# Packing, gated heads and merged branches moved between the weight blocks of a hybrid decoder layer

## The chip, the cores and the metric

The kernel runs on one core of a Trainium2 chip. The time is the device's, in microseconds, of one execution; the figure to be predicted is the median of several executions. TensorE (PE) does the matmuls, VectorE (DVE) and ScalarE (ACT) casts, sums and activations, GpSimd (POOL) and SyncE (SP) issue DMAs. Each engine works its own instructions in order and waits on semaphores of the others.

## The reference

One layer, x of 256 rows and 4096 columns, all in fp32:

- pre-RMSNorm, then one projection `hn @ w_in`, whose 18336 columns are split among two attention branches, two gate paths (2048 columns each) and two merge gates (`merge_a`, `merge_b`, 4096 columns each);
- branch A (latent attention) and branch B (sparse attention with an indexer) give `o_a` and `o_b`, 256 x 2048 each, multiplied by the SiLU of their gates;
- `merged = sigmoid(merge_a) * (o_a @ p_a) + sigmoid(merge_b) * (o_b @ p_b)`;
- the result is `x + merged @ w_o`.

The weights are 4096 x 18336 (`w_in`), 2048 x 4096 (`p_a`, `p_b`) and 4096 x 4096 (`w_o`), beside two smaller ones.

## The kernel before

Every fp32 matrix is split into two fp32r parts, `hi` (a cast on ACT) and `lo` (the rest, a subtraction on DVE), and a product is three matmuls of 128 x 128 by 128 x 512: hi by hi, lo by hi, hi by lo (`mm3`, lines 105 to 108). So each block of weights is loaded by SP, cast by ACT, subtracted by DVE, and then multiplied by PE.

**The streams** (`run_streams`). Up to 1215 us the columns of `w_in` for the branches and gates, and the first 1024 of `merge_a`, go through PE in streams of 512 columns. A stream has 16 weight units of two 128-row tiles; one unit is 12 matmuls for the two halves of x. At a unit the casts and subtractions of the unit two ahead are issued (`hi_part`, `lo_part`; three buffers of each, so a cast waits until PE has released a buffer), and the load of the one six ahead (four buffers). After the first tile of a unit a hook `each(u)` may issue more work. The last two streams, `done_ma(0)` and `done_ma(1)`, are the first 1024 columns of `merge_a`; their results go through a sigmoid on ACT (L1096) and by POOL to `sig_d` in HBM (L1087).

**The wide units.** From there on work is a list `sched` of units, written out by `block(w, c0, order, end)`: an order is a list of unit names, 1024 columns wide.

- `p5` is a plain unit: weight rows of tiles 10 and 11, four quarters (two halves of the rows, two of the columns) x 2 tiles x 3 = 24 matmuls.
- `s4` does the tiles 8 and 9 with Strassen's products: 7 x 3 = 21 matmuls. It needs sums of the weights (three DVE operations, L1195 to L1197, into `wsum`, a single buffer) and more casts; and sums of the left matrix, which were "packed" before: for each chunk `c` of four 128-row tiles, `a_sums` (L1070 to L1073) makes three sums and overwrites one quarter, and the sums are split into `xh`, `xl`. An s unit of tiles 2p, 2p+1 uses chunk p/2.
- `g` loads gated heads of a branch from `go_d`, `m` merged columns from `mt_d`, both through the weights' ring, and split two chunks into the tiles `h` and `l` that held x or the heads before; `m` also packs. `d` does that for the last merged columns, straight from SBUF. `t` transposes the merged result of a p_a/p_b block (16 short matmuls, four ACT copies). None of g, m, d has matmuls of its own.

The order of work is written out by hand. For unit i (`run_wide`), DVE's and ACT's work of unit i+2 is issued first (`prep`), then SP's loads of units i+3 to i+5 (`raw_dma`, a ring `wraw` of three buffers of 1 MB, used by s, p, g and m), then PE's products of unit i, then the block's `end`. Of `whi` and `wlo` there are three buffers, of `whs` and `wls` (for s units) two.

The blocks: seven of `w_in` (the rest of the merge gates; results through sigmoids to `sig_d`), alternately four of `p_a` and four of `p_b`, four of `w_o`. The gate blocks use x; the units of `p_a` use chunks 0 to 3 (g0, g1), those of `p_b` chunks 4 to 7 (g2, g3); those of `w_o` chunks 0 to 7 (m0: 0, 1; m1: 2, 3; m2: 4, 5; d3: 6, 7). In the last gate block g0 and g1 stand among the units; in the first p_a block g2 and g3; in the last p_b block m0 and m1; in the first w_o block m2, t3 and d3. POOL loads the sigmoids of a p block at its first unit (`on_first`, `load_sig`, 1 MB), into a buffer of `whs`.

**Packing x** for the gate blocks: `pack_x(c)`, at every second unit of the last stream (`each_pack`), one chunk at a time, in `wsum`. The sigmoids of the two merge streams are also written to `wsum`.

**The end.** A block has four accumulators for the quarters (`banks_c`) and four for Strassen's products (`banks_s`). `sets` says which are the four single-bank tiles ("c": `tr`, `tr`, `at`, `at`) and which the two tiles of two banks each ("s": `acc`). After the last s unit the Strassen products are summed (`sums_early`); after the last p unit each quarter is added (`sum_late`, L1257). In the last block x is added by an accumulating DMA of POOL (`add_x`, L1341) between the two, and each quarter leaves by SP as soon as it is added.

Of the kernel before, what the change touches and what calls it, by code (L numbers as in the profile page):

```python
# [9 lines left out]
F32 = mybir.dt.float32  # L10
F32R = mybir.dt.float32r
# [7 lines left out]
P = 128  # L19
# [18 lines left out]
def kernel(ctx: ExitStack, tc: tile.TileContext, x, positions, g_pre, w_in, g_q_lat,  # L38
# [79 lines left out]
    def flat(t):  # L118
        return t.rearrange("p a t -> p (a t)")
# [917 lines left out]

    F = {"h": xth, "l": xtl, "xh": [], "xl": []}  # L1040
# [16 lines left out]
    def sum_tiles(c):
        for q, lst in (("xh", F["xh"]), ("xl", F["xl"])):
            t = F["px"].tile([P, 3, P], F32R, name=f"{q}{c}")
            if len(lst) > c:  # L1060
                lst[c] = t
            else:
                lst.append(t)

    def a_sums(sums, a):

        v = nc.vector.tensor_tensor
        a11, a21, a12, a22 = (a[:, q * P:(q + 1) * P] for q in range(4))
        s1, s2, s4 = (sums[:, q, :] for q in range(3))
        v(s1, a21, a22, op=ALU.add)  # L1070
        v(a21, a21, a11, op=ALU.subtract)
        v(s2, s1, a11, op=ALU.subtract)
        v(s4, a12, s2, op=ALU.subtract)  # L1073

    def pack_x(c):

        t = flat(wsum())
        a, sums = t[:, 0:512], t[:, 512:896].rearrange("p (q t) -> p q t", q=3)
        nc.vector.tensor_tensor(a, flat(xth[c][:, 0:2, :]).bitcast(F32), flat(xtl[c][:, 0:2, :]).bitcast(F32),
                                op=ALU.add)  # L1080
        a_sums(sums, a)
        sum_tiles(c)
        split_w(xth[c][:, 0, P:], xtl[c][:, 0, P:], a[:, P:2 * P])
        split_w(F["xh"][c], F["xl"][c], sums)

    def out_sig(d, sg, b):
        nc.gpsimd.dma_start(sig_d[d][:, 512 * b:512 * b + 512].rearrange("(m p) c -> p m c", p=P), sg)  # L1087
# [1 line left out]
    def done_ma(b):  # L1089
        def done(acc):  # L1090
            if b == 0:
                yield from idle()
                open_wide()
            sg = wsum()[:, 0:2, :]
            for m in range(2):
                nc.scalar.activation(sg[:, m, :], acc[:, m, :], AF.Sigmoid, scale=r[:, m:m + 1])  # L1096
            release("acc")
            out_sig(0, sg, b)
            yield
        return done  # L1100

    def each_pack(u):
        if u % 2 == 1:
            pack_x(u // 2)


    for b in range(2):
        stream(stat_x, w_in, [(C_MA + 512 * b, 512)], done_ma(b), each=each_pack if b else None)


    sched = []
# [32 lines left out]
    def raw_dma(i):  # L1144
        if i >= len(sched) or i in asked:
            return
        asked.add(i)
        u = sched[i]
        kind, p, b = u["kind"], u["p"], u["b"]
        if kind not in "spgm":  # L1150
            return
        t = raws[i] = F["pa"].tile([P, 4, 512], F32, name="wraw", bufs=3)
        if kind in "gm":
            src = go_d[p // 2][:, 8 * (p % 2):8 * (p % 2) + 8, :] if kind == "g" else mt_d[:, 8 * p:8 * p + 8, :]
            nc.sync.dma_start(flat(t), src.rearrange("p k t -> p (k t)"))
            return
        for kk in range(2):
            q = 1 - kk if kind == "s" else kk
            row = (2 * p + kk) * P
            nc.sync.dma_start(flat(t[:, 2 * q:2 * q + 2, :]), b["w"][row:row + P, b["c0"]:b["c0"] + 1024])  # L1160

    def new_a(c):
        F["h"][c] = big.tile([P, 4, S], F32R, name=f"h{c}")
        F["l"][c] = big.tile([P, 4, S], F32R, name=f"l{c}")
        return F["h"][c], F["l"][c]

    def prep(i):

        if i >= len(sched) or i in his:
            return  # L1170
        u = sched[i]
        kind, p = u["kind"], u["p"]
        his[i] = None
        if kind == "t":
            return
        if kind in "gmd":
            raw = flat(F["merged_t"] if kind == "d" else raws[i])
            for q in range(2):
                c = (4 * (p // 2) + 2 * (p % 2) if kind == "g" else 2 * p) + q
                h, l = new_a(c)  # L1180
                a = raw[:, 1024 * q:1024 * q + 1024]
                if kind != "g":
                    sums = wsum()[:, 0, 0:384].rearrange("p (q t) -> p q t", q=3)
                    a_sums(sums, a)
                    sum_tiles(c)
                    split_w(F["xh"][c], F["xl"][c], sums)
                split_w(flat(h), flat(l), a)
# [90 lines left out]
    for n, (d, cb) in enumerate(gates):  # L1278
        order = mixed
        if n == 0:  # L1280
            order = "p1 p3 s0 p5 s2 p7 s4 p9 s6 p11 s8 s10 p13 s12 s14 p15".split()
        if n == len(gates) - 1:
            order = mixed[:6] + ["g0"] + mixed[6:10] + ["g1"] + mixed[10:]
        block(w_in, (C_MA, C_MB)[d] + 1024 * cb, order, end_sig(d, 1024 * cb))


# [48 lines left out]

# [21 lines left out]
    first_of = {}
    for i, u in enumerate(sched):
        if u["b"] is not None:
            first_of.setdefault(id(u["b"]), i)  # L1360

    def on_first(i, u):
        b = u["b"]
        if b["w"] is p_a or b["w"] is p_b:
            d = 0 if b["w"] is p_a else 1
            F["sig", d] = load_sig(d, b["c0"] // 1024)

    def run_wide():
        F["pb"] = ctx.enter_context(tc.tile_pool(name="wide2", bufs=1, side="right"))
        for i, u in enumerate(sched):  # L1370
            b = u["b"]
            if b is not None and first_of[id(b)] == i:
                on_first(i, u)
            prep(i + 2)
            for j in range(3, 6):
                raw_dma(i + j)
# [86 lines left out]
```

## Time and profile before

| | us |
|---|---|
| median of 3 executions | 2509.92 (2507.33 to 2510.38) |
| profiled execution, its own time | 2511.02 |
| its span, first to last instruction | 2509.1 |
| PE busy | 2476.4 (99%) |
| DVE busy | 1800.9 (72%) |
| ACT busy | 1318.7 (53%) |
| mean granted TensorE clock | 0.994 |

Matmuls overlap, so "PE busy" says that PE had something to do, not that it ran at full pace; the pace is seen in the number of matmuls of a stretch. The stretches: streams to about 1215 us, gate blocks to 1797, p_a and p_b to 2153, w_o to the end. In a row of the windows view the columns are the stretch, its length, and for each engine busy time and number of instructions, then the granted clock (1.00 is 2.4 GHz, 0.5 is 1.2), the DMA engines' share and GB/s. In a row of a timeline: start, duration, engine, line, operation, written and read tiles, shape, count, and in brackets the idle time of the engine before it and what ended it.

### The profile page before, as it was taken

The numbers are of one execution on the slowest core, as the hardware profiler recorded it, in microseconds if no ns is written. First come the engines' busy times: TensorE is split into PE (matmuls) and PEld (weight loads), VectorE is DVE, ScalarE is ACT, GpSimd is POOL, SyncE is SP. The second block draws the span as 40 slices with busy tenths as digits, with TensorE's granted clock in tenths as the row PEclk, the third lists the DMA queues.
The fourth block names the chain that finished last, engine by engine and source line by source line (L and its number), as shares of the span: only waits on it lengthen the run. The fifth ranks groups of instructions, "written<-read, shape, count | busy, mean of one in ns | idle before, by whom it ended". The sixth has DMA issues, their size and how long they took to land.

```text
span 2509.1 us, 31278 instructions
## 1 busy us (share of the span) xinstructions
PE 2476.4 (99%) x11790; PEld 2066.0 (82%) x11790; DVE 1800.9 (72%) x2086; ACT 1318.7 (53%) x1618; POOL 114.0 (5%) x159
## 2 busy tenths in 40 slices
PE   9999999999999999999999999999999999989998
PEld 7988888888888888887788888888788888768887
DVE  5676696655666666655899998999845456799996
ACT  6555545555665555553455555556533334455553
POOL 2000000000000000000000000000000000000000
PEclk9999999999999999999999999999999999999999
DMA  7655565565666666666556666666867666657775
GB/s 244 187 170 160 162 182 163 167 183 176 179 192 179 187 179 188 180 178 193 204 200 241 219 218 213 215 228 216 289 231 239 206 225 234 202 173 246 237 233 151
DMA packets 202790, 506.18 MB, mean 202 GB/s; under 512 B 25428, under 2 KB 38608, under 8 KB 201360
## 3 DMA queue, kind: packets, MB, share of 16 engines
q1 hardware_dynamic: 190816, 468.25, 59.2%
q0 software_dynamic: 11776, 35.93, 4.6%
q8 instruction: 92, 1.51, 0.2%
q14 instruction: 58, 0.48, 0.1%
q10 hardware_dynamic: 48, 0.02, 0.0%
HBM read 482.11 MB, written 22.02 MB: 201 GB/s over the span
## 4 chain that ended last, share of the span: by engine, by line
PE 83%; issue 9%; DMA 3%; DVE 3%; ACT 1%; SPq 0%; POOL 0%; DVEq 0%; ACTq 0%; POOLq 0%
PE acc L108 18%; PE acc L106 18%; PE acc L107 18%; PE at L108 4%; PE at L107 4%; PE at L106 4%; PE tr L106 4%; PE tr L107 4%; PE tr L108 4%; PE tr L129 2%; DVE wlo L1052 1%; DMA ev<-in_x 1%; DVE wls L1052 1%; DMA wraw<-in_p_a 1%; PE tr L615 0%
## 5 line engine op out<-in xcount | busy, mean ns | idle before, releaser
L237 DVE TENSOR_TENSOR lo<-raw,hi 128x1024 fp32r<-128x1024 f32 (+3 forms) x400 | 476.2, 1192 | 373.8 <-ACT hi L229 358.3
L1051 ACT CAST whi<-wraw 128x1536 fp32r<-128x1536 f32 (+1 forms) x240 | 419.6, 1755 | 458.9 <-PE at L107 232.2
L1052 DVE TENSOR_TENSOR wlo<-wraw,whi 128x1536 fp32r<-128x1536 f32 (+1 forms) x240 | 502.1, 2093 | 217.4 <-ACT whi L1051 217.1
L106 PE MATMUL acc<-hi,h 128*128 128x512 f32 (+1 forms) x1404 | 555.2, 395 | 2.4 <-ACT hi L229 1.9
L229 ACT CAST hi<-raw 128x1024 fp32r<-128x1024 f32 (+3 forms) x400 | 407.4, 1023 | 283.9 <-PE acc L107 256.7
L108 PE MATMUL acc<-lo,h 128*128 128x512 f32 (+1 forms) x1404 | 546.8, 389 | 0.5 <-DVE lo L237 0.5
L107 PE MATMUL acc<-hi,l 128*128 128x512 f32 (+1 forms) x1404 | 545.3, 388 | 0.8 <-DVE l L85 0.8
L108 PEld LDWEIGHTS acc<-lo,h 128*128 128x128 f32 x1404 | 263.8, 188 | 56.6 <-DVE lo L237 1.0
L106 PEld LDWEIGHTS acc<-hi,h 128*128 128x128 f32 x1404 | 264.0, 188 | 49.9 <-ACT hi L229 2.3
L107 PEld LDWEIGHTS acc<-hi,l 128*128 128x128 f32 x1404 | 264.3, 188 | 48.4 <-DVE l L85 1.1
L106 PE MATMUL acc<-whi,h 128*128 128x512 f32 x600 | 236.4, 394 | 7.4 <-DVE ev L1257 5.3
L108 PE MATMUL acc<-wlo,h 128*128 128x512 f32 x600 | 235.6, 393 | 3.2 <-DVE wlo L1052 3.2
L107 PE MATMUL acc<-whi,l 128*128 128x512 f32 x600 | 235.2, 392 | 0.0
L1051 ACT CAST whs<-wsum 128x1536 fp32r<-128x1536 f32 x88 | 130.3, 1480 | 119.4 <-DVE wsum L1196 119.3
L108 PE MATMUL tr<-wlo,h 128*128 128x512 f32 x440 | 171.4, 390 | 1.6 <-DVE wlo L1052 1.6
L106 PE MATMUL tr<-whi,h 128*128 128x512 f32 x440 | 171.7, 390 | 0.0
L107 PE MATMUL tr<-whi,l 128*128 128x512 f32 x440 | 171.6, 390 | 0.0
L1052 DVE TENSOR_TENSOR wls<-wsum,whs 128x1536 fp32r<-128x1536 f32 x88 | 154.2, 1752 | 1.2 <-PE acc L108 1.2
L106 PEld LDWEIGHTS acc<-whi,h 128*128 128x128 f32 x600 | 113.9, 190 | 32.9 <-DVE ev L1257 6.5
L106 PE MATMUL at<-whi,h 128*128 128x512 f32 x352 | 136.9, 389 | 0.0
L107 PE MATMUL at<-whi,l 128*128 128x512 f32 x352 | 136.9, 389 | 0.0
L108 PE MATMUL at<-wlo,h 128*128 128x512 f32 x352 | 136.9, 389 | 0.0
(333 smaller groups left out, 3480.8 us busy)
## 6 DMA issues: line engine op xcount, KB each, us to landing
raw<-in_w_in SPq DMA_DIRECT2D x335, 512.0 KB, 3.7
wraw<-in_w_in SPq DMA_DIRECT2D x224, 512.0 KB, 4.6
wraw<-in_w_o SPq DMA_DIRECT2D x128, 512.0 KB, 5.1
wraw<-in_p_a SPq DMA_DIRECT2D x64, 512.0 KB, 4.9
wraw<-in_p_b SPq DMA_DIRECT2D x64, 512.0 KB, 5.1
raw<-in_w_uq SPq DMA_DIRECT2D x32, 384.0 KB, 3.2
raw<-in_w_ukv SPq DMA_DIRECT2D x16, 512.0 KB, 4.1
whs<-sig_d POOLq DMA_DIRECT2D x16, 512.0 KB, 6.4
```

What stands on the lines that cost most here:

```text
L106: nc.tensor.matmul(o, ah, bh, start=start, stop=False)
L107: nc.tensor.matmul(o, al, bh, start=False, stop=False)
L108: nc.tensor.matmul(o, ah, bl, start=False, stop=stop)
L129: nc.tensor.transpose(tr[:, a * S + m * P:a * S + (m + 1) * P], src_of(a, m), ident)
L229: nc.scalar.copy(t[:, ks, :width(i)], raws[i][:, ks, :width(i)])
L237: nc.vector.tensor_tensor(t[:, ks, :wd], raws[i][:, ks, :wd], his[i][:, ks, :wd].bitcast(F32), op=ALU.subtract)
L1051: nc.scalar.copy(hi, src)
L1052: nc.vector.tensor_tensor(lo, src, hi.bitcast(F32), op=ALU.subtract)
```

## The change

- The two merge streams go over the weight units in the order 0, 2, ..., 14, 1, 3, ..., 15.
- x is packed two chunks at a time, four times, at the units 4, 10, 1 and 7 of the second stream (the third, sixth, ninth and twelfth in its order), in a buffer of the weights' ring `wraw`. The sigmoids of the merge streams are written to a buffer of that ring too.
- For g and m, both chunks are summed and cast together: all casts on ACT first, then all subtractions on DVE. The sums `xh`, `xl` of two chunks share a tile.
- g0 moves behind s14 of the last gate block, g1 behind p0 of the first p_a block, g2 behind its p4, g3 behind p1 of the first p_b block. The sigmoids of a p block are loaded at its unit p2.
- m2 moves into the last p_b block; t3 and d3 come later in the first w_o block; d3 packs chunk 6 alone, chunk 7 is packed by a new unit k7 after p3 of the second w_o block, and s14 of the first w_o block becomes p14.
- The last w_o block starts with p1 and p3, and has `sets` "cs" for "sc".

```diff
-    def pack_x(c):
-        t = flat(wsum())
...
+    def pack(cs, t):
+        n = len(cs)
+        a = t[:, 0:512 * n].rearrange("p (c q t) -> p c q t", c=n, q=4)
+        sums = t[:, 512 * n:896 * n].rearrange("p (c q t) -> p c q t", c=n, q=3)
+        for i, c in enumerate(cs):
+            nc.vector.tensor_tensor(t[:, 512 * i:512 * i + 512], flat(F["h"][c][:, 0:2, :]).bitcast(F32),
+                                    flat(F["l"][c][:, 0:2, :]).bitcast(F32), op=ALU.add)
         a_sums(sums, a)
...
+        for i, c in enumerate(cs):
+            nc.scalar.copy(F["h"][c][:, 0, P:], a[:, i, 1, :])
+        nc.scalar.copy(xh, sums)
+        for i, c in enumerate(cs):
+            nc.vector.tensor_tensor(F["l"][c][:, 0, P:], a[:, i, 1, :], F["h"][c][:, 0, P:].bitcast(F32),
+                                    op=ALU.subtract)
+        nc.vector.tensor_tensor(xl, sums, xh.bitcast(F32), op=ALU.subtract)
+    def wraw():
+        return F["pa"].tile([P, 4, 512], F32, name="wraw", bufs=3)
...
-            sg = wsum()[:, 0:2, :]
+            sg = wraw()[:, 0:2, :]
...
     def each_pack(u):
-        if u % 2 == 1:
-            pack_x(u // 2)
+        cc = {4: 0, 10: 1, 1: 2, 7: 3}.get(u)
+        if cc is not None:
+            pack((2 * cc, 2 * cc + 1), flat(wraw()))
...
+        units_b = stream(stat_x, w_in, [(C_MA + 512 * b, 512)], done_ma(b), each=each_pack if b else None, now=False)
+        plan += units_b[::2] + units_b[1::2]
...
+        if kind == "k":
+            pack((p,), flat(wsum()))
+            return
...
+                n = 1 if kind == "d" else 2
+                sums = flat(wsum())[:, 0:384 * n].rearrange("p (c q t) -> p c q t", c=n, q=3)
+                a_sums(sums, raw.rearrange("p (c q t) -> p c q t", c=2, q=8)[:, 0:n])
+                xh, xl = sum_tiles(p)
+                parts.insert(0, (xh[:, 0:n], xl[:, 0:n], sums))
+            for hi, _, src in parts:
+                nc.scalar.copy(hi, src)
+            for hi, lo, src in parts:
+                nc.vector.tensor_tensor(lo, src, hi.bitcast(F32), op=ALU.subtract)
...
-            order = mixed[:6] + ["g0"] + mixed[6:10] + ["g1"] + mixed[10:]
+            order = mixed[:15] + ["g0", "p15"]
...
-            oa[3:3] = ["g3"]
-            oa[1:1] = ["g2"]
+            oa = "p0 g1 p1 p2 p3 p4 g2 p5 p6 p7".split()
+            ob = "p0 p1 g3 p2 p3 p4 p5 p6 p7".split()
...
-            ob = "p0 m0 p1 p2 p3 m1 p4 p5 p6 p7".split()
+            ob = "p0 m0 p1 p2 m1 p3 p4 p5 m2 p6 p7".split()
...
-            order = ("p1 p3 m2 p5 t3 p7 s0 p9 s2 d3 s4 p11 s6 s8 p13 s10 s12 s14 p15").split()
-        block(w_o, 1024 * cb, order, end_out if cb < 3 else None, sets="sc")
+            order = "p1 p3 t3 p5 p7 d3 s0 p9 s2 s4 p11 s6 s8 p13 s10 s12 p14 p15".split()
+        elif cb == 1:
+            order = mixed[:4] + ["k7"] + mixed[4:]
+        elif cb == 3:
+            order = "p1 p3 s0 p5 s2 p7 s4 p9 s6 p11 s8 s10 p13 s12 s14 p15".split()
+        block(w_o, 1024 * cb, order, end_out if cb < 3 else None, sets="sc" if cb < 3 else "cs")
...
-        if b["w"] is p_a or b["w"] is p_b:
+        if u["p"] == 2 and (b["w"] is p_a or b["w"] is p_b):
             d = 0 if b["w"] is p_a else 1
             F["sig", d] = load_sig(d, b["c0"] // 1024)
```

## Rows read from the trace of the kernel before

**Rows 1.** The page's busy times: engine, busy us, share of the span, instructions.
```profile
PE 2476.4 (99%) x11790; PEld 2066.0 (82%) x11790; DVE 1800.9 (72%) x2086; ACT 1318.7 (53%) x1618; POOL 114.0 (5%) x159
```

**Rows 2.** Busy time of each engine in stretches of the span (windows view).
```profile
1178.00:1240.00 62.00, 53.45 (x214) 42.44 (x214) 49.59 (x78) 31.36 (x40) 0.73 (x1) 0.92 0.55 191
1240.00:1740.00 500.00, 500.00 (x2207) 414.03 (x2206) 460.90 (x395) 277.43 (x227) 13.00 (x24) 1.00 0.63 218
1740.00:1820.00 80.00, 76.68 (x336) 62.43 (x335) 67.44 (x55) 46.83 (x37) 4.31 (x8) 1.00 0.79 277
...
2160.00:2262.00 102.00, 92.01 (x383) 73.31 (x382) 92.54 (x93) 54.17 (x50) 3.58 (x4) 0.93 0.54 178
...
2496.00:2509.10 13.10, 6.18 (x18) 4.32 (x18) 2.83 (x5) 0.00 (x0) 1.37 (x2) 0.85 0.68 150
```

**Rows 3.** Timeline of PE from 1179.5 to 1185 us.
```profile
1179.96 0.50 PE L106 MATMUL acc<-hi,h 128*128 128x512 f32 x1 [1.88 <-ACT hi L229]
...
1181.81 0.63 PE L106 MATMUL acc<-hi,h 128*128 128x512 f32 x1
1182.24 0.63 PE L107 MATMUL acc<-hi,l 128*128 128x512 f32 x1
...
1184.25 0.40 PE L106 MATMUL acc<-hi,h 128*128 128x512 f32 x1
```

**Rows 4.** The chain that ended last: start, length, work.
```profile
1169.77 6.66 DMA sig_d<-wsum
...
1223.90 3.07 DMA sig_d<-wsum
...
1800.98 11.28 DMA wraw<-in_p_a
```

**Rows 5.** Timeline of DVE from 1170.8 to 1190 us.
```profile
1176.54 0.69 DVE L1079 TENSOR_TENSOR wsum<-h,l 128x512 f32<-128x512 f32 x1 [4.50 <-DMA sig_d<-wsum]
1177.27 0.29 DVE L1070 TENSOR_TENSOR wsum<-wsum 128x128 f32<-128x128 f32 x1
...
1185.62 2.36 DVE L237 TENSOR_TENSOR lo<-raw,hi 128x1024 fp32r<-128x1024 f32 x2 [0.40 <-ACT hi L229]
```

**Rows 6.** Timeline of DVE from 2150 to 2168 us.
```profile
2152.14 0.68 DVE L1305 TENSOR_TENSOR whs<-tr,whs 128x512 f32<-128x512 f32 x1
...
2157.45 0.28 DVE L1070 TENSOR_TENSOR wsum<-wraw 128x128 f32<-128x128 f32 x1
...
2165.74 4.49 DVE L1052 TENSOR_TENSOR wlo<-wraw,whi 128x2048 fp32r<-128x2048 f32 x2 [0.57 <-ACT whi L1051]
```

**Rows 7.** Timeline of ACT from 1169 to 1190 us.
```profile
1169.74 1.05 ACT L229 CAST hi<-raw 128x1024 fp32r<-128x1024 f32 x1 [0.51 <-PE acc L107]
...
1184.12 0.51 ACT L1051 CAST xh<-wsum 128x384 fp32r<-128x384 f32 x1 [0.23 <-DVE wsum L1073]
```

**Rows 8.** The page's DMA issues: tiles, issuer, count, KB each, median us to landing.
```profile
wraw<-in_w_in SPq DMA_DIRECT2D x224, 512.0 KB, 4.6
```

**Rows 9.** Timeline of DVE from 2212 to 2224 us: an s unit, then a p unit.
```profile
2213.37 1.22 DVE L1195 TENSOR_TENSOR wsum<-wraw 128x1024 f32<-128x1024 f32 x1
...
2219.90 2.28 DVE L1052 TENSOR_TENSOR wlo<-wraw,whi 128x2048 fp32r<-128x2048 f32 x1
```

**Rows 10.** Timeline of POOL from 1780 to 1802 us.
```profile
1781.54 1.07 POOL L1290 DMA_DIRECT2D whs<-sig_d  x2 [57.52 <-PE at L107]
1797.70 2.38 POOL L1271 DMA_DIRECT2D sig_d<-ev  x4 [15.09 <-ACT ev L1270]
1800.08 1.07 POOL L1290 DMA_DIRECT2D whs<-sig_d  x2
```

**Rows 11.** Timeline of DVE from 2490 us to the end.
```profile
2497.66 0.69 DVE L1257 TENSOR_TENSOR ev<-acc,ev 128x512 f32<-128x512 f32 x1 [2.63 <-DMA ev<-in_x]
...
2505.40 0.76 DVE L1257 TENSOR_TENSOR ev<-acc,ev 128x256 f32<-128x256 f32 x2 [1.76 <-PE acc L108]
```

**Rows 12.** The four x additions of the last block (L1341, from 2485 us).
```profile
DMA to landing us min/median/max: 4.3/6.4/8.0
```

More of the change, by code (lines that the diff above doesn't have):

```diff
@@ L1026 @@
     gate("a", 3)
-    F = {"h": xth, "l": xtl, "xh": [], "xl": []}
+    F = {"h": xth, "l": xtl, "xh": {}, "xl": {}}
     QUARTERS = [(m, h) for m in range(2) for h in range(2)]
@@ L1055, in wsum, with sum_tiles @@
         return F["pa"].tile([P, 3, 512], F32, name="wsum")
[L1057 to L1063, printed above, removed]
+    def sum_tiles(cc):
+        hl = [F["px"].tile([P, 2, 3, P], F32R, name=f"{q}{cc}") for q in ("xh", "xl")]
+        F["x2", cc] = hl
+        for q in range(2):
+            F["xh"][2 * cc + q], F["xl"][2 * cc + q] = hl[0][:, q], hl[1][:, q]
+        return hl
     def a_sums(sums, a):
         v = nc.vector.tensor_tensor
-        a11, a21, a12, a22 = (a[:, q * P:(q + 1) * P] for q in range(4))
-        s1, s2, s4 = (sums[:, q, :] for q in range(3))
+        a11, a21, a12, a22 = (a[:, :, q, :] for q in range(4))
+        s1, s2, s4 = (sums[:, :, q, :] for q in range(3))
         v(s1, a21, a22, op=ALU.add)
@@ L1073, in a_sums @@
         v(s4, a12, s2, op=ALU.subtract)
-    def pack_x(c):
-        t = flat(wsum())
-        a, sums = t[:, 0:512], t[:, 512:896].rearrange("p (q t) -> p q t", q=3)
-        nc.vector.tensor_tensor(a, flat(xth[c][:, 0:2, :]).bitcast(F32), flat(xtl[c][:, 0:2, :]).bitcast(F32),
-                                op=ALU.add)
-        a_sums(sums, a)
-        sum_tiles(c)
-        split_w(xth[c][:, 0, P:], xtl[c][:, 0, P:], a[:, P:2 * P])
-        split_w(F["xh"][c], F["xl"][c], sums)
+    def pack(cs, t):
[5 more added lines that the diff above has]
+                                    flat(F["l"][c][:, 0:2, :]).bitcast(F32), op=ALU.add)
+        a_sums(sums, a)
+        if n == 2:
+            xh, xl = sum_tiles(cs[0] // 2)
+        else:
+            xh, xl = (q[:, cs[0] % 2:cs[0] % 2 + 1] for q in F["x2", cs[0] // 2])
+        for i, c in enumerate(cs):
[7 more added lines that the diff above has]
+        return F["pa"].tile([P, 4, 512], F32, name="wraw", bufs=3)
     def out_sig(d, sg, b):
@@ L1102, in each_pack @@
     def each_pack(u):
-        if u % 2 == 1:
-            pack_x(u // 2)
+        cc = {4: 0, 10: 1, 1: 2, 7: 3}.get(u)
+        if cc is not None:
+            pack((2 * cc, 2 * cc + 1), flat(wraw()))
     for b in range(2):
-        stream(stat_x, w_in, [(C_MA + 512 * b, 512)], done_ma(b), each=each_pack if b else None)
+        units_b = stream(stat_x, w_in, [(C_MA + 512 * b, 512)], done_ma(b), each=each_pack if b else None, now=False)
+        plan += units_b[::2] + units_b[1::2]
     sched = []
@@ L1151, in raw_dma @@
             return
-        t = raws[i] = F["pa"].tile([P, 4, 512], F32, name="wraw", bufs=3)
+        t = raws[i] = wraw()
         if kind in "gm":
@@ L1175, in prep @@
             return
+        if kind == "k":
+            pack((p,), flat(wsum()))
+            return
         if kind in "gmd":
             raw = flat(F["merged_t"] if kind == "d" else raws[i])
[L1178 to L1187, printed above, removed]
+            c0 = 4 * (p // 2) + 2 * (p % 2) if kind == "g" else 2 * p
+            hl = [new_a(c0 + q) for q in range(2)]
+            parts = [(flat(hl[q][0]), flat(hl[q][1]), raw[:, 1024 * q:1024 * q + 1024]) for q in range(2)]
+            if kind != "g":
+                n = 1 if kind == "d" else 2
[7 more added lines that the diff above has]
+                nc.vector.tensor_tensor(lo, src, hi.bitcast(F32), op=ALU.subtract)
             return
@@ L1213, in unit_s @@
         b, c = u["b"], u["p"] // 2
-        h, l, xh, xl = (flat(F[q][c]) for q in ("h", "l", "xh", "xl"))
+        h, l = flat(F["h"][c]), flat(F["l"][c])
+        xh, xl = flat(F["xh"][c]), flat(F["xl"][c])
         bh, bl, th, tl = his[i], los[i], hits[i], lots[i]
@@ L1353, with on_unit @@
         if cb == 0:
-            order = ("p1 p3 m2 p5 t3 p7 s0 p9 s2 d3 s4 p11 s6 s8 p13 s10 s12 s14 p15").split()
-        block(w_o, 1024 * cb, order, end_out if cb < 3 else None, sets="sc")
[L1357 to L1362, printed above, removed]
+            order = "p1 p3 t3 p5 p7 d3 s0 p9 s2 s4 p11 s6 s8 p13 s10 s12 p14 p15".split()
[4 more added lines that the diff above has]
+        block(w_o, 1024 * cb, order, end_out if cb < 3 else None, sets="sc" if cb < 3 else "cs")
+    def on_unit(u):
         b = u["b"]
-        if b["w"] is p_a or b["w"] is p_b:
+        if u["p"] == 2 and (b["w"] is p_a or b["w"] is p_b):
             d = 0 if b["w"] is p_a else 1
@@ L1371, in run_wide @@
             b = u["b"]
-            if b is not None and first_of[id(b)] == i:
-                on_first(i, u)
+            if b is not None:
+                on_unit(u)
             prep(i + 2)
```

## The prediction

> **What bounds the kernel now.** I read the busy times first: TensorE (PE) is busy 2476 of 2509 us [rows 1], so only what PE loses can be won. A busy PE can still be a slow one, so next I counted its matmuls by stage. In 1240 to 1740 us it runs 2207 in 500 us: 0.2266 us each, its full pace [rows 2]. Against that, four stretches fall short. 1178 to 1240: 214 x 0.2266 = 48.5, so 13.5 us are lost. 1740 to 1820: 336 x 0.2266 = 76.1, 3.9 lost. 2160 to 2262: 383 records, 16 of them the short transposes of one t unit (1.7 us together, an estimate from a matmul of a quarter of the columns with some start-up); 367 x 0.2266 + 1.7 = 84.9, 17.1 lost. 2496 to the end: 18 x 0.2266 = 4.1 of 13.1, 9.0 lost or tail. Those 43 us are all that this change can reach; DVE is 92% busy in the 500 us where PE loses nothing, so a busy DVE alone is no loss.
>
> The PE timeline at the first of them shows what a loss is made of: a wait of 1.9 us, and then matmuls that start 0.43 us apart, not 0.23 [rows 3]; nine steps from start to start take 4.29 us where full pace needs 2.04, so this loss is 1.9 + 2.25 = 4.1. The granted clock is 0.92 over that stretch [rows 2]: PE at half its pace (1.2 for 2.4 GHz) for some us after a long wait. The stretch from 1740 to 1820 loses 3.9 us with the clock at 1.00: shorter waits there did not bring it.
>
> **What the waits come from.** The chain shows two sigmoid stores of 6.66 and 3.07 us, and one weight load of 11.28 us [rows 4]. Behind the first store stands DVE: it idles 4.50 us until the store of the sigmoids has left `wsum`, because the first packing of x wants the same single buffer [rows 5]. ACT and DVE work in order, so the casts of the next weights stand behind it. The second store holds `wsum` against unit s0's sums in the same way. The third stretch is DVE's: after the last p_b block it does the four merges (5.3 us), then m2 with its two chunks one after the other (8.3 us until the next cast, 2157.45 to 2165.74), and only then the weights of p5 [rows 6], which PE had already asked for.
>
> **The change, part by part.**
>
> *Sigmoids into the weights' ring, and x packed two chunks at a time.* The store's buffer is now another than the packing's, so the 4.50 us go, and with them the half pace behind them. What comes new is a longer burst: four packings of two chunks (third, sixth, ninth and twelfth weight unit) for eight of one. Is it covered? A unit here is 12 matmuls, 2.72 us; casts run two units ahead. With T the PE start of the unit, ACT's cast (1.05) and DVE's subtraction follow its release, and the packing starts on DVE at T + 2.2 (the next instruction starts 1.13 after the subtraction) [rows 5, 7]: two subtractions take 2.36, so one takes 1.23. The trace has no such operation from SBUF at widths of 256 or 768. Bounds: 256 lies between the 128 (0.29) and the 512 (0.69) [rows 5]; 768 on ACT between 384 (0.51) and 1024 (1.05) [rows 7]. I take 0.42, near the half of the last two 256-wide ones from PSUM (0.76 for both [rows 11]), and 0.83, on the line through its bounds. Two adds (0.60 and 0.73 from start to start, the second being waited for), four sums (0.46, 0.34, 0.46, then 0.42 to the end), ACT's 768-wide cast (its successor may start 0.74 after it), ACT's weight cast (1.05), DVE's subtraction (1.23): 0.60 + 0.73 + 1.68 + 0.04 + 0.74 + 1.07 + 1.23 = 6.1 us; 5.2 with the low bounds, 7.4 with the high. PE wants that subtraction by T + 3 x 2.72 + 2 matmuls = T + 8.6; it is there at T + 8.3. The next packing starts 8.24 after the first, against three units of 8.16: 0.08 lost each time, 0.3 of slack used up. So no wait, or tenths: I take 0.3 for all four; by the bounds 0 to 4 x 1.1 = 4.4.
>
> *Start of the wide units.* The last packing used to sit behind the first two weight casts; now it is four units earlier, and s0's `wsum` is free. But the ring gives up two early loads: s0's weights wait until p1's are split (before, all three were asked for at once), and s2's until the second sigmoid store has landed. Walking the queues on (PE ends the streams at about 1210.6; p1 and p3 take 24 matmuls, 5.44 each; a wide load lands in 4.6 [rows 8]): p1 split at 1209.3, s0's weights there at 1214.5, its sums, casts and subtractions need 6.1 of the 6.53 that an s unit takes on DVE [rows 9], so ready at 1220.6; PE wants it at 1221.4. s2: store out by 1218.7 with the longer 6.66, weights by 1223.3, ready by 1229.8; wanted at 1231.6. Covered, by 0.8 and 1.8 us. Of 13.5 lost I take 13 as gone (9 if the bounds above fall badly).
>
> *Gated heads.* g0 and g1 leave the middle of the last gate block (one DVE and ACT burst of 2.4 less among s units) and go before its last p, and into the p blocks, where DVE has 2.3 us of work per unit [rows 9] and PE 5.44. Walked through: p0 of p_a is split at 9.0 after s14 begins and wanted at 10.2; p1 at 15.3 against 15.6, plus two matmuls. The sigmoid loads move from a block's first unit to its third. On POOL's queue that puts the first of them behind the four sigmoid stores, not ahead of them [rows 10], and since POOL waits for no PE there, the second block's load follows at once: 1 MB of stores and 2 MB of loads together. The load of 11.28 us fell among 1 MB and 1 MB. In the new order the weights at risk are p4's: asked for at 16.3 after s14, wanted at 32.0; 16.3 + 11.3 + 1.9 + 2.3 = 31.8. Of 3.9 I take 3.5 as gone; none to all by the bounds.
>
> What the row shows is a weight load that takes 11.28 for 4.6 us while POOL's transfers are queued [rows 4, 8]. The Trainium skill (DMA: Bandwidth & Descriptors, "Queues, rings and completion order") says that each DMA engine takes packets from its queues in turn, so POOL's megabytes halve the weights' share for as long as they last. The row agrees, for two megabytes. By that rule the third makes the load later still, and the sum 2.6 us worse (rival B, priced from rows); by the row as it stands, nothing.
>
> *Merged branches.* m2 moves into the last p_b block, where its weights' copy has room, and two chunks are now done in one go: sums 1.7, then three casts, two subtractions: about 5.9 for 8.3. w_o's first block keeps t3 and half of d3 (chunk 7's sums go to k7 in the second block, and s14 becomes p14: 3 matmuls more, 0.7 us). DVE's bill in this block: end of p_b 5.3, d3 about 5, seven s at 6.53 and nine p at 2.3 [rows 9], 3.3 for the early sums: 80 us. PE's: nine p, seven s of 21 matmuls, 1.7 for t3: 84. In step: p5 split 7.7 after p_b's end (wanted at 12.5), p7 at 9.9 (18.0), d3 done 18.4, s0 ready 24.3 (23.5 and two matmuls: 0.4 late), then s4 0.25, s8 0.2, s12 0.2, the evacuation before the second block 0.3, s4 behind k7 0.7: 2.0 us of short waits, no half pace. I count 17.1 - 2.0 - 0.7 = 14.4 gained; down to 6 if DVE slips half a us per unit, up to 16.
>
> *Last block.* The accumulators of the final products were two pairs of banks; a read of one bank held PE off its neighbour, so PE waited for the first x addition (DVE starts at 2497.66, idle until its DMA) [rows 11] and then ran at half pace. With "cs" the four quarters lie in four tiles and PE ends near 2499. But the end is then set by the last of the four additions, which take 4.3 to 8.0 us [rows 12]: the fourth, issued at about 2495.9, lands at 2503.9; 0.43 on DVE, then the store as now. DVE's last pair starts at 2505.40 today [rows 11], so 1.5 us are gained of 9 (0 to 2).
>
> *Sum.* 13 - 0.3 + 3.5 + 14.4 + 1.5 = 32.1 us, 31 to 33 with rounding. The profiled execution took 2511.0, its span 2509.1; the median of the runs is 2509.9, 1.1 less than it. 2509.9 - 32.1 = 2477.8.
>
> **Rivals.**
> A. DVE stays the bound in w_o's first block. For: 92.5 of 102 us busy there now [rows 2]; the bill of 80 against 84 leaves 4 for every wait on ACT. Against: 13 us of its work leave the block. If each of 16 units slips 0.5: 8 us more, 2486.
> B. Loads come late. If POOL's megabytes delay a weight load in proportion (two made it 6.7 late [rows 4, 8]), three make p4's take 4.6 + 1.5 x 6.7 = 14.6: 0.8 and 1.8 us of waits. And s0's load behind the store, 2 us later, brings a loss like that at 1180, 4.1. Together 2484.5. For: 11.28. Against: p_a's loads have the slack of two g units less than before.
> C. The waits only move, since no work is taken away and ACT, DVE and PE are coupled: 2510. For: DVE's work is the same. Against: the 500 us with DVE at 92% and no wait.
> D. Slower. The pairs are bursts that a look-ahead of two units doesn't cover: it decides once a pair takes 0.3 us over my 6.1. Then four packings, m0 to m2, d3 and k7 each cost a loss of 4.1 with its half pace: 37 against the 32 removed, 2515. Against: m0 and m1 run unpaired, at 8.3, without a loss now.
>
> **How the numbers follow.** My forecast 0.60 (its own range 2473 to 2482), A 0.15, B 0.13, C 0.06, D 0.06. A and B together give 2492.5. The good ends of all bounds, 13.5 + 3.9 + 16 + 2, give 2474.5, and the runs scatter by 3 us. So 2471 to 2493. This kernel's measurements tell 0.2% (5 us) from no change: faster is 0.60 + 0.15 + 0.13 = 0.88, same C, slower D.
>
> **What would show it.** No DVE wait for a DMA out of `wsum`; PE at full pace from 1178 to 1240; waits of tenths after each pair, if any; after p_b's end no wait for p5's weights, some below 0.7 us at s units; PE's clock full until the last block's end; the last store behind the last x addition. Wrong if: PE shows half pace after a pair (D), if the waits at w_o are over 1 us each (A), or if ACT waits for weight loads at p4 or s0 (B).

## The result, and the profile after

The changed kernel takes 2476.5 us (median of 4 runs, 2476.3 to 2477.4) against 2510.1 (2507.3 to 2510.4) for the kernel before on the same chip: 0.9869 of its time, 95% interval 0.9852 to 0.9886. Forecast were 2477.8 us and 2471 to 2493. Its span is 2474.7 us for 2509.1, the mean granted clock 0.999 for 0.994.

The page's busy times after, which answer to [rows 1]:

```profile
PE 2460.9 (99%) x11793; PEld 2058.9 (83%) x11793; DVE 1791.5 (72%) x2048; ACT 1317.4 (53%) x1610; POOL 113.9 (5%) x159
```

PE is 99% busy in both, so this row shows neither the fault nor the gain. The windows view does; these are the stretches of [rows 2] (the last one moved with the end), with the same columns:

```profile
1178.00:1240.00 62.00, 62.00 (x274) 51.03 (x274) 55.88 (x62) 35.90 (x37) 0.73 (x1) 1.00 0.64 221
1240.00:1740.00 500.00, 500.00 (x2208) 414.01 (x2207) 464.12 (x398) 279.14 (x228) 13.02 (x24) 1.00 0.64 220
1740.00:1820.00 80.00, 79.59 (x352) 65.58 (x351) 58.18 (x44) 41.82 (x32) 4.27 (x8) 1.00 0.78 281
2160.00:2262.00 102.00, 101.80 (x448) 83.56 (x447) 100.59 (x92) 55.37 (x46) 5.80 (x8) 1.00 0.70 230
2460.00:2474.70 14.70, 5.62 (x25) 4.32 (x23) 4.38 (x8) 0.00 (x0) 3.33 (x4) 0.83 0.68 143
```

Between 1178 and 1240 us PE now runs 274 matmuls for 214, which is 0.2263 us each: full pace, nothing lost. 1740 to 1820: 352 for 336. 2160 to 2262: 448 in 102 us, full pace again, and the clock is 1.00 where it was 0.92 and 0.93. DVE is busy for 100.6 of those 102 us and PE still loses next to nothing. Only the end kept its loss: 25 matmuls are 5.7 of 14.7 us.

For the account I took the start of every matmul in both traces and added up what each step exceeds the pace of 0.227 us by. Sums of such steps are called PE's loss below.

| term | forecast gain | PE's loss before and after | what undoing it cost, on the chip |
|---|---|---|---|
| start of the wide units | 13 - 0.3 | 4.3 + 1.9 + 7.7, then 0 | e1: 5.5, e2: 1.8 |
| gated heads | 3.5 | 1.12 + 3.02, then 0.67 | e5: 4.2 |
| merged branches | 14.4 | 6.2 + 7.5 + 0.5 + 2.9, then 0.7 (and 0.7 for p14) | e12: 14.3 |
| last block | 1.5 | 6.3, then 0, but the tail behind PE grew by 5.4 | e4: 1.3 |
| sum | 32.1 | 13.9 + 3.5 + 15.7 + 0.9 = 34.0 | |

The spans differ by 34.4 us, the medians by 33.6.

**The packing pair.** DVE's timeline after, which answers to [rows 5]:

```profile
1174.37 1.29 DVE L1081 TENSOR_TENSOR wraw<-h,l 128x512 f32<-128x512 f32 x2
1175.69 0.42 DVE L1070 TENSOR_TENSOR wraw<-wraw 128x256 f32<-128x256 f32 x1
...
1178.27 0.96 DVE L1094 TENSOR_TENSOR xl<-wraw,xh 128x768 fp32r<-128x768 f32 x1 [0.50 <-ACT xh L1090]
1179.21 3.50 DVE L237 TENSOR_TENSOR lo<-raw,hi 128x1024 fp32r<-128x1024 f32 x3
1182.62 1.29 DVE L1081 TENSOR_TENSOR wraw<-h,l 128x512 f32<-128x512 f32 x2
```

No wait for a store stands ahead of the first row, where 4.50 us stood. From its start to the end of the first weight subtraction behind the pair (1179.21 + 1.23) are 6.07 us, forecast 6.1; the next pair starts 8.25 us after the first, forecast 8.24. The 256-wide sum takes the 0.42 us that was chosen between 0.29 and 0.69.

**The p blocks.** POOL's timeline after ([rows 10] before), then from the views of single lines what three groups took to land: the first four loads of the sigmoids, the two of p4's weights, and the two of p5's:

```profile
1783.88 2.38 POOL L1294 DMA_DIRECT2D sig_d<-ev  x4 [74.01 <-ACT ev L1293]
1786.25 2.11 POOL L1313 DMA_DIRECT2D whs<-sig_d  x4
```

```profile
DMA to landing us min/median/max: 12.3/15.7/18.5
```

```profile
DMA to landing us min/median/max: 7.7/8.7/9.8
```

```profile
DMA to landing us min/median/max: 8.1/9.1/10.0
```

As forecast, both blocks' loads follow the stores at once, 3 MB together. They land late, but nobody waits for them. p4's weights come in 9.8 us, not in the 11.3 that was copied from [rows 4] or the 14.6 of rival B: asked for by 1787.2, they are split at 1801.3, 2.1 us before p4's first matmul at 1803.4. What is left of PE's waits in the wide units are these two groups (total us, times, longest):

```profile
PE acc L108 <- DVE wlo L1052: 0.4, 1, 0.4
PE at L108 <- DVE wls L1052: 0.2, 1, 0.2
```

The first is p5's. Its weights were asked for only at 1795.0, when p3's had been split; by 1795.3 the last of POOL's stores had landed, so their 10.0 us fell beside the sigmoid loads alone, and behind g2's load in SP's own queue. The second is that of s4 in the second w_o block, behind k7.

**The first w_o block.** DVE after ([rows 6] before), and the whole of the block in the windows view:

```profile
2139.77 2.28 DVE L1052 TENSOR_TENSOR wlo<-wraw,whi 128x2048 fp32r<-128x2048 f32 x1
2143.14 2.29 DVE L1052 TENSOR_TENSOR wlo<-wraw,whi 128x2048 fp32r<-128x2048 f32 x1 [1.08 <-ACT whi L1051]
2147.91 0.29 DVE L1070 TENSOR_TENSOR wsum<-wls 128x128 f32<-128x128 f32 x1 [2.49 <-ACT wls L1342]
...
2153.02 1.22 DVE L1217 TENSOR_TENSOR wsum<-wraw 128x1024 f32<-128x1024 f32 x1
```

```profile
2136.00:2221.00 85.00, 85.00 (x383) 70.22 (x382) 79.45 (x73) 47.50 (x41) 0.00 (x0) 1.00 0.56 187
```

PE ends p_b at 2135.8. p5's weights are split at 2142.1 (6.3 later, forecast 7.7), p7's at 2145.4 (9.7, forecast 9.9), d3 is done at 2153.1 (17.3, forecast 18.4). DVE's bill, forecast 80 us, is 79.45 in this window; since DVE works up to two units ahead of PE, the window does not hold exactly the work of the bill.

In the kernel before, the largest single loss of this block, 7.5 us, stood before s4: DVE did d3's two chunks one after the other (from the first row) and only then s4's sums (the second).

```profile
2190.48 0.29 DVE L1070 TENSOR_TENSOR wsum<-wls 128x128 f32<-128x128 f32 x1
...
2198.12 1.22 DVE L1195 TENSOR_TENSOR wsum<-wraw 128x1024 f32<-128x1024 f32 x1
```

**The end.** DVE's last rows, which answer to [rows 11], PE's last matmul, and the landing of the four x additions ([rows 12] before):

```profile
2464.19 0.69 DVE L1280 TENSOR_TENSOR ev<-tr,ev 128x512 f32<-128x512 f32 x1 [2.60 <-DMA ev<-in_x]
2467.83 0.69 DVE L1280 TENSOR_TENSOR ev<-tr,ev 128x512 f32<-128x512 f32 x1 [2.95 <-DMA ev<-in_x]
2469.11 0.69 DVE L1280 TENSOR_TENSOR ev<-at,ev 128x512 f32<-128x512 f32 x1 [0.59 <-DMA ev<-in_x]
2471.00 0.76 DVE L1280 TENSOR_TENSOR ev<-at,ev 128x256 f32<-128x256 f32 x2 [1.20 <-DMA ev<-in_x]
```

```profile
2465.23 0.39 PE L108 MATMUL at<-wlo,h 128*128 128x512 f32 x1
```

```profile
DMA to landing us min/median/max: 4.3/6.8/8.5
```

PE ends at 2465.6; before, three of DVE's four waits were for PE, now all four are for the additions. From PE's end to the end of the span are 9.1 us, before 3.7: of the 6.3 us that PE won there, 5.4 were given back.

### The profile page after: what moved, and what is told of

It reads as the page before. It is cut to its first block, busy times and chain, and to the rows that moved or that the text cites. A ratio compares the mean times of both kernels' runs of the same rounds, so it can differ in the third digit from the quotient of the medians.

```text
span 2474.7 us, 31244 instructions
## 1 busy us (share of the span) xinstructions
PE 2460.9 (99%) x11793; PEld 2058.9 (83%) x11793; DVE 1791.5 (72%) x2048; ACT 1317.4 (53%) x1610; POOL 113.9 (5%) x159
## 4 chain that ended last, share of the span: by engine, by line
PE 85%; issue 8%; DMA 3%; DVE 3%; ACT 0%; POOL 0%; SPq 0%; DVEq 0%; ACTq 0%; POOLq 0%
PE acc L106 19%; PE acc L108 19%; PE acc L107 18%; PE at L106 4%; PE at L107 4%; PE at L108 4%; PE tr L107 4%; PE tr L106 4%; PE tr L108 4%; PE tr L129 2%; DMA ev<-in_x 1%; DVE wlo L1052 1%; DVE wls L1052 1%; DMA wraw<-in_p_a 1%; DMA out<-ev 1%
## 5 line engine op out<-in xcount | busy, mean ns | idle before, releaser
L108 PE MATMUL acc<-wlo,h 128*128 128x512 f32 x543 | 211.4, 389 | 0.4 <-DVE wlo L1052 0.4
L106 PE MATMUL acc<-whi,h 128*128 128x512 f32 x543 | 211.6, 390 | 0.0
L107 PE MATMUL acc<-whi,l 128*128 128x512 f32 x543 | 211.3, 389 | 0.0
L106 PE MATMUL tr<-whi,h 128*128 128x512 f32 x471 | 183.2, 389 | 0.0
L107 PE MATMUL tr<-whi,l 128*128 128x512 f32 x471 | 183.2, 389 | 0.0
L108 PE MATMUL tr<-wlo,h 128*128 128x512 f32 x471 | 183.2, 389 | 0.0
L106 PE MATMUL at<-whi,h 128*128 128x512 f32 x384 | 149.4, 389 | 0.0
L107 PE MATMUL at<-whi,l 128*128 128x512 f32 x384 | 149.4, 389 | 0.0
L108 PE MATMUL at<-wlo,h 128*128 128x512 f32 x384 | 149.4, 389 | 0.0
L108 PEld LDWEIGHTS acc<-wlo,h 128*128 128x128 f32 x543 | 101.9, 188 | 22.0 <-DVE wlo L1052 0.8
```

The source lines that it names most:

```text
L106: nc.tensor.matmul(o, ah, bh, start=start, stop=False)
L107: nc.tensor.matmul(o, al, bh, start=False, stop=False)
L108: nc.tensor.matmul(o, ah, bl, start=False, stop=stop)
```

## The experiments

The theory: PE waits because DVE is late, and DVE is late because of the buffer shared with the store (start), of bursts in the wrong places (gated heads, merged branches), of work done chunk by chunk, and in the p blocks of weights that land late. The rivals: the pairing is what counts, wherever it stands; or the places count and the pairing is worth nothing. Differences are taken from the changed kernel's 2476.5 us; each ratio is against the kernel before on the same chip, with its 95% interval. Of these chips only that of e9 to e11 ran the changed kernel again. Where the kernel before was fastest (e1 to e4, 2507.0 us), ratios would make each difference some 2.5 us larger. I go by the times: the changed kernel gave 2476.5 us both times it was measured, and PE's loss in the runs' own traces supports them.

**e1: sigmoids in `wsum` again.**

```diff
-            sg = wraw()[:, 0:2, :]
+            sg = wsum()[:, 0:2, :]
```

> The changed kernel, with the sigmoids of the merge streams in wsum again (packing in pairs stays in the ring). Theory (each loss had its own cause, here the buffer that the store holds): no loss at the first packing, since that no longer uses wsum; s0's sums wait for the second store, which lands at 1218.4 in the changed kernel, so they start 7 us later than there, s0 is ready near 1224.6 for 1221.3 wanted: 3 us of wait, with half pace behind it 4 to 6 us: 2481 to 2483. Rival (the pairs, not the buffer, made the gain): within 0.5 us of 2476.5.

2482.0 us, 0.9901 (0.9886 to 0.9916): 5.5 more, PE's loss 5.5 at 1221 to 1229 us. DVE and PE there:

```profile
1219.36 1.23 DVE L1217 TENSOR_TENSOR wsum<-wraw 128x1024 f32<-128x1024 f32 x1 [8.26 <-DMA sig_d<-wsum]
```

```profile
1222.93 0.50 PE L106 MATMUL acc<-whs,xh 128*128 128x512 f32 x1 [1.61 <-ACT whs L1051]
1223.27 0.40 PE L107 MATMUL acc<-whs,xl 128*128 128x512 f32 x1
1225.44 0.79 PE L108 MATMUL acc<-wls,xh 128*128 128x512 f32 x1 [1.77 <-DVE wls L1052]
1226.03 0.63 PE L106 MATMUL acc<-whs,xh 128*128 128x512 f32 x1
1226.45 0.63 PE L107 MATMUL acc<-whs,xl 128*128 128x512 f32 x1
```

s0's sums wait 8.26 us for the store; PE waits 1.6 and 1.8 us and then goes at half pace (0.43 from start to start). Only the second store matters here: the first holds `wsum` too, but the packing now uses the ring.

**e2: x packed one chunk at a time, at every second unit in its natural order, in `wsum`; the sigmoids stay in the ring.**

```diff
-        cc = {4: 0, 10: 1, 1: 2, 7: 3}.get(u)
...
+        if u % 2 == 1:
+            c = u // 2
...
+            pack((c,), flat(wsum()))
...
-        plan += units_b[::2] + units_b[1::2]
+        plan += units_b
```

> The changed kernel, with x packed one chunk at a time at every second unit in wsum, in the natural order of units, as before; the sigmoids stay in the ring. Theory: no loss at 1180 (DVE needs 5.67 us per two units of 5.44, a lag of 1.6 over seven packings, for a slack of 1.8); the last packing again stands behind the casts of p1 and p3, which costs the 1.9 us of 1215 and some of s0: 2 to 4 us, 2478.5 to 2480.5. Rival (the pairs made the gain): 9 us or more, 2485.5.

2478.4 us, 0.9885 (0.987 to 0.990): 1.8 more. PE's loss is 1.7, one wait at 1212.5 us, where the last packing stands again behind the first wide units; none at 1180. Of the 13.9 us that were lost at the start, the store's other buffer alone brings 12.2; pairs and order bring the rest. The two are no fixed shares: in e1 the packing's other buffer ends the first wait without it, and pairs, order and that buffer alone bring 8.4.

**e7: the pairs at every second unit for every third.**

```diff
-        cc = {4: 0, 10: 1, 1: 2, 7: 3}.get(u)
+        cc = {4: 0, 8: 1, 12: 2, 1: 3}.get(u)
```

> The changed kernel with the four paired packings at every second unit (third, fifth, seventh, ninth) and not at every third. Theory (a pair just fits three units: 8.26 for 8.16): over two units DVE needs 7.1 for 5.44, 1.7 late at each of the last three after 0.3 of slack: 4 to 5 us of waits, 2481, and more if PE falls to half pace. Rival (the look-ahead hides such bursts): within 1 us of 2476.5.

2481.4 us, 0.9894 (0.9879 to 0.9908): 4.9 more. PE's waits from 1170 to 1215 us:

```profile
PE acc L106 <- ACT hi L229: 1.6, 3, 0.6
PE acc L108 <- DVE lo L237: 1.6, 3, 0.5
```

Two units are 5.44 us and a pair needs 7.1 from pair to pair; the deficit is met bit by bit, and with waits of at most 0.6 us the clock stays at 1.00. The spacing of three units is what makes the pair free.

**e5: g0 to g3 and the load of the sigmoids at their old places.**

```diff
-            order = mixed[:15] + ["g0", "p15"]
+            order = mixed[:6] + ["g0"] + mixed[6:10] + ["g1"] + mixed[10:]
...
-            oa = "p0 g1 p1 p2 p3 p4 g2 p5 p6 p7".split()
-            ob = "p0 p1 g3 p2 p3 p4 p5 p6 p7".split()
+            oa[3:3] = ["g3"]
+            oa[1:1] = ["g2"]
...
-        if u["p"] == 2 and (b["w"] is p_a or b["w"] is p_b):
+        if u["p"] == 0 and (b["w"] is p_a or b["w"] is p_b):
```

> The changed kernel with g0 to g3 and the sigmoid loads at their places of before. Theory: the losses of the stretch from 1740 to 1820 come back, 3.0 to 3.9 us: 2479.5 to 2480.5. Rival (loads are late either way, since the same bytes are moved): within 1 us of 2476.5.

2480.7 us (2480.2 to 2483.7), 0.9889 (0.9873 to 0.9906): 4.2 more. The profiled execution is the slowest of the four, and PE fell to half pace in it (clock 0.96 from 1740 to 1820 us), which the kernel before did not do here [rows 2]. e5 undoes the places and the moment of the sigmoid loads together; what each is worth no run here shows.

**e3: the merged branches at their old places (three in w_o's first block), but two chunks at a time.**

```diff
-            ob = "p0 m0 p1 p2 m1 p3 p4 p5 m2 p6 p7".split()
+            ob = "p0 m0 p1 p2 p3 m1 p4 p5 p6 p7".split()
...
-            order = "p1 p3 t3 p5 p7 d3 s0 p9 s2 s4 p11 s6 s8 p13 s10 s12 p14 p15".split()
-        elif cb == 1:
-            order = mixed[:4] + ["k7"] + mixed[4:]
+            order = "p1 p3 m2 p5 t3 p7 s0 p9 s2 d3 s4 p11 s6 s8 p13 s10 s12 s14 p15".split()
...
-                n = 1 if kind == "d" else 2
+                n = 2
```

> The changed kernel with m1, m2, t3 and d3 at their places of before, d3 with both chunks, no k7, s14 for p14; two chunks are still done in one go. Theory (DVE's order and load behind p_b's end): 14.4 less the 2 to 4 us by which the pairs are shorter: 10 to 12 us, 2487 to 2489, with the clock at half again. Rival (the pairs made the gain, the places do nothing): within 1.5 us of 2476.5.

2484.9 us, 0.9913 (0.9898 to 0.9928): 8.4 more, less than expected (by PE's loss in its trace, with p14's 0.7 set off, 9.2). PE in this stretch:

```profile
2176.56 0.50 PE L106 MATMUL at<-whs,xh 128*128 128x512 f32 x1 [1.54 <-ACT whs L1051]
2176.90 0.40 PE L107 MATMUL at<-whs,xl 128*128 128x512 f32 x1
2179.07 0.50 PE L108 MATMUL at<-wls,xh 128*128 128x512 f32 x1 [1.77 <-DVE wls L1052]
2179.40 0.40 PE L106 MATMUL at<-whs,xh 128*128 128x512 f32 x1
```

The waits are back, but the half pace is not: the last two start 0.33 us apart, and those behind them 0.23. The expected half pace did not come; the rival (the places do nothing) is refuted.

**e8: the new places, but m0 to m2 chunk after chunk.**

```diff
+            if kind == "m":
+                xh, xl = sum_tiles(p)
+                for q in range(2):
+                    sums = flat(wsum())[:, 0:384].rearrange("p (c q t) -> p c q t", c=1, q=3)
+                    a_sums(sums, raw.rearrange("p (c q t) -> p c q t", c=2, q=8)[:, q:q + 1])
+                    split_w(xh[:, q:q + 1], xl[:, q:q + 1], sums)
+                    split_w(*parts[q])
+                return
```

> The changed kernel with the two chunks of m0 to m2 done one after the other, as before, at the new places. Theory (the place matters, the pair saves 2.4 us of DVE where there is room): 0 to 1 us, 2476.5 to 2477.5. Rival (the pairs made the gain at the end of p_b): 4 us or more.

2480.1 us, 0.9887 (0.9872 to 0.9902): 3.6 more where at most 1 was expected. A pair after (first fence) takes 6.3 us from its first sum to the next unit's subtraction, chunk after chunk in e8 (second fence) 8.3; the third fence is PE's wait in e8:

```profile
2113.88 0.42 DVE L1070 TENSOR_TENSOR wsum<-wraw 128x256 f32<-128x256 f32 x1
...
2120.17 2.29 DVE L1052 TENSOR_TENSOR wlo<-wraw,whi 128x2048 fp32r<-128x2048 f32 x1 [0.40 <-ACT whi L1051]
```

```profile
2100.44 0.29 DVE L1070 TENSOR_TENSOR wsum<-wraw 128x128 f32<-128x128 f32 x1
...
2108.74 4.49 DVE L1052 TENSOR_TENSOR wlo<-wraw,whi 128x2048 fp32r<-128x2048 f32 x2 [0.58 <-ACT whi L1051]
```

```profile
PE tr L108 <- DVE wlo L1052: 2.0, 2, 1.4
```

So the pairing counts inside p_b too: all three m units in that block are covered at 6.3 us; at 8.3, m1 and m2 are not.

**e9: old places and chunk after chunk; e12: the same with d3 chunk after chunk too.** The edits are those of e3 and e8; in e12 the condition of e8's branch is `kind != "g"`.

> The merged branches as in the kernel before in both respects: at the old places and chunk after chunk. Theory (the old places and the missing pairs each cost, and together they give the forecast 14.4 less the 0.7 for p14): 2476.5 + 8.4 (old places with pairs, measured) + 3.5 to 6 = 2488 to 2491, and the half pace of the stretch around 2165 to 2178 is back, because the wait before p5's weights is again longer than 2 us. Rival (the two add, no more: what is lost is the DVE time of the unpaired work, whatever the place): 2476.5 + 8.4 + 3.5 = 2488.4 with no half pace. Rival (the old places alone are the loss): 2485, as with pairs. 2485 +- 1 refutes the first two.

> All merged branches, d3 too, at the old places and chunk after chunk: the whole treatment of before within the changed kernel. Theory (the rest of what the third stretch gained is d3's pairing): 2 to 3 us above the run with d3 paired, 2490.5 to 2491.5, with TensorE's loss at about 2180 to 2190 us grown from 5.5 towards the 7.5 of the kernel before. Rival (d3's pairing is worth nothing, and the rest of the gain came with something else): 2488.5.

e9: 2488.5 us, 0.9915 (0.990 to 0.9929), 12.0 more; places (8.4) and pairs (3.6) add up, within runs of each that scatter by 2 to 3.5 us. The time fits the theory and its first rival alike; the clock decides, for half pace is back. PE's waits for p5's weights in e9:

```profile
2147.93 0.50 PE L106 MATMUL acc<-whi,h 128*128 128x512 f32 x1 [1.26 <-ACT whi L1051]
...
2150.26 0.51 PE L108 MATMUL acc<-wlo,h 128*128 128x512 f32 x1 [1.59 <-DVE wlo L1052]
```

They are as long as in the kernel before, and neither is over 2 us, as the expectation had it. e12: 2490.8 us, 0.9927 (0.9913 to 0.994), 14.3 more. The first w_o block of both in the windows view, e9 first:

```profile
2140.00:2242.00 102.00, 93.18 (x397) 74.57 (x396) 93.95 (x92) 56.30 (x50) 3.57 (x4) 0.97 0.55 180
```

```profile
2140.00:2242.00 102.00, 92.01 (x383) 73.33 (x383) 91.64 (x95) 53.34 (x48) 3.35 (x4) 0.93 0.51 172
```

e12 is the row of [rows 2] again: 383 matmuls in 102 us, clock 0.93. It lies 2.3 us above e9, on another chip and with runs from 2488.8 to 2492.2; PE's loss at 2180 to 2190 us, 7.5 for 5.5 in e9, says the same of d3's pairing. With e12 the whole term is reproduced from its parts: 14.3 us by the medians, for a forecast of 14.4, and 15.7 in the profiled execution, the slowest of the six, as in the account above.

**e4: the last block's order and accumulators as before.**

```diff
-        elif cb == 3:
-            order = "p1 p3 s0 p5 s2 p7 s4 p9 s6 p11 s8 s10 p13 s12 s14 p15".split()
-        block(w_o, 1024 * cb, order, end_out if cb < 3 else None, sets="sc" if cb < 3 else "cs")
+        block(w_o, 1024 * cb, order, end_out if cb < 3 else None, sets="sc")
```

> The changed kernel with the last block as before: order s0 p1 s2 ..., accumulators of the quarters in the two-bank tiles. Theory: PE waits 3.4 us for the first x addition and falls to half pace, yet the end, set by the fourth x addition, moves by 1 to 2 us only: 2477.5 to 2478.5. Rival (PE's wait is what the end pays): 6 us, 2482.5.

2477.8 us, 0.9883 (0.9867 to 0.990): 1.3 more. PE's wait of before is back, and half pace behind it:

```profile
2465.51 0.50 PE L106 MATMUL acc<-whi,h 128*128 128x512 f32 x1 [3.44 <-DVE ev L1280]
...
2467.37 0.63 PE L106 MATMUL acc<-whi,h 128*128 128x512 f32 x1
2467.79 0.63 PE L107 MATMUL acc<-whi,l 128*128 128x512 f32 x1
```

```profile
2472.59 0.76 DVE L1280 TENSOR_TENSOR ev<-acc,ev 128x256 f32<-128x256 f32 x2 [1.75 <-PE acc L108]
```

e4 undoes order and accumulators together. 6.4 us of PE, and 1.3 of the time: the last sum (second fence, DVE) comes at 2472.59 behind PE, and in the changed kernel at 2471.00 behind the fourth x addition.

**e6, e10, e11: x of the last block loaded ahead by SP into a buffer of the ring, and added by DVE.** e6 and e11 are one kernel; e10 is the changed kernel, run beside e11.

```diff
+            if i == len(sched) - 4:
+                xt = F["x_last"] = wraw()
+                for m in range(2):
+                    nc.sync.dma_start(flat(xt[:, 2 * m:2 * m + 2, :]), xf[m * P:(m + 1) * P, 3072:4096])
...
-                        for q in QUARTERS:
-                            add_x(b, *q)
+                        for m, h in QUARTERS:
+                            nc.vector.tensor_tensor(b["ev"][m, h], b["ev"][m, h], F["x_last"][:, 2 * m + h, :], op=ALU.add)
```

> The changed kernel; in the last block x is loaded by SP some 15 us ahead into a free buffer of the weights' ring and added by DVE (four additions) behind the early sums; no accumulating DMA there. Theory (the end is set by the fourth x addition by DMA): the last quarters are added when PE is done, 4.5 us sooner: 2472. Rival (the end is set by the stores' own time, up to 6 us when they queue): 0 to 1 us sooner.

> The changed kernel once more, unedited, beside the next run on the same chip: 2476 to 2477.5 us.

> The x of the last block loaded ahead and added by DVE, once more, beside the changed kernel on the same chip. Theory (the end is set by the fourth accumulating transfer of x, and DVE can add x in its place at 0.69 us a piece): 3.5 to 4.5 us below the changed kernel, 2472 to 2473. Rival (the difference seen was one between chips): within 1 us of it.

e6: 2472.8 us, 0.9859 (0.9844 to 0.9874). e10: 2476.5 us (2475.8 to 2476.9), 0.9867 (0.9852 to 0.9882). e11: 2471.7 us (2471.5 to 2474.9), 0.9852 (0.9836 to 0.9869): 4.8 less than e10, with no overlap of the runs. DVE's end in e11:

```profile
2461.20 2.49 DVE L1414 TENSOR_TENSOR ev<-ev,wraw 128x512 f32<-128x512 f32 x4
2463.61 1.29 DVE L1280 TENSOR_TENSOR ev<-tr,ev 128x512 f32<-128x512 f32 x2
2464.80 1.35 DVE L1280 TENSOR_TENSOR ev<-at,ev 128x512 f32<-128x512 f32 x3
```

Four additions take 2.49 us where the transfers took 4.3 to 8.5 each, and from the first of them DVE waits for nothing. The span ends at 2469.7, 4.4 us after PE. So what the last block gave back is to be had: this is the fastest version here.

## Why the prediction was right

- **The shared buffer.** Right, and the largest single thing: the 4.50 us wait and both half-pace stretches are gone. e1 and e2 separate it from the pairing. The pair itself came out at 6.07 us for 6.1, so rival D had no ground; e7 shows that it was close: a denser spacing costs 4.9 us. The 0.3 us of waits charged for the pairs did not come; PE shows none of 0.1 us there.
- **Start of the wide units.** The result was right, a step of the walk was not. s0's weights were to be asked for at 1209.3, when p1 was split; they were asked for at 1204.0, when the fourth packing gave its buffer back, and landed by 1209.7. s0's sums start at 1211.3. The loss is 0, not 0.5.
- **Gated heads.** Right in the sum, 3.5. p4's weights, forecast 0.2 us ahead of PE, were 2.1 ahead, mainly since the load was mis-sized: 9.8 us with three megabytes in POOL's queue, not the 11.3 of two, nor the 14.6 of rival B. The sign given for B, ACT waiting for p4's load, did show (4.4 us) and cost PE nothing. The walk stopped one unit short: p5's weights came 0.4 us late. The Trainium skill (DMA: Bandwidth & Descriptors, "Queues, rings and completion order") says that each DMA engine takes turns among the queues that have work, a packet at a time. From that I estimate that a load's share depends on whether the other queue has packets, not on how many megabytes wait in it, which is not how the prediction read the rule; the rows agree with this reading, 9.8 for 11.3.
- **Merged branches.** Bill and walk were right (79.45 for 80; p5, p7 and d3 0.2 to 1.4 us earlier than walked). Mis-sized were the short waits: 2.0 us were charged, 0.7 came. d3 was done 1.1 us earlier than walked, and the lags of 0.2 to 0.4 at s0, s4 and s8 lay within that. Those at s12 (0.3, forecast 0.2) and behind k7 (0.5, forecast 0.7) stayed. The cause given was incomplete: m2 ahead of p5's weights was 6.2 of the 17.1 us lost there, and the largest loss, 7.5, stood before s4, behind d3. The change moved d3 too, so the term came out all the same. Rival A's premise holds (DVE is busy for 100.6 of 102 us), its price does not.
- **Last block.** Right that the end would be set by the fourth x addition, and that PE's gain would mostly be lost: 0.9 to 1.3 us for 1.5.
- **Missed.** The argument against rival D, that m0 and m1 run chunk after chunk without a loss, held for the old order alone: e8 shows 3.6 us at the new places. And e3 was put at 10 to 12 us, with half pace, for 8.4 without.

## To carry over

A store that leaves from the scratch buffer of the next step makes that step wait for the whole transfer; look for the idle row that ends with a store before counting instructions, since giving the store another buffer was worth up to 12 of 34 us here. Work that has no matmuls of its own is free only where the gap to the next such piece exceeds its chain of engines (pairs of 6.1 us at 8.2 cost nothing, at 5.4 they cost 4.9 us). Freeing the busiest engine at the end of a kernel is worth only what the transfer behind it allows: 6.3 us of PE became 1 us, until the transfer went too.

## What was not expected

Half pace does not follow from the length of a wait alone. In e1, PE waits 1.61 and 1.77 us with two matmuls between, and the next steps are 0.43 us; in e3 it waits 1.54 and 1.77 us with two matmuls between, and the pace stays at 0.23. In e9 waits of only 1.26 and 1.59 us bring half pace again. What decides between them no run here shows.

Four accumulating transfers of 256 KB, issued within 2.6 us, land later one after the other: 4.3 us after its issue the first, 8.5 the last, though nothing but these and the stores of the results is under way. Four DVE additions of the same data took 2.49 us (e11), once x had been loaded.
